# A decoder step in fp32 on one core: the sampled tokens' output projection and second MLP product as unsplit matmuls in two column tiles, with their weights in the ring of gathered keys

## The chip, the cores and the metric

The kernel runs on one core of a Trainium2 chip. TensorE (PE) multiplies, VectorE (DVE), ScalarE (ACT) and GpSimd (POOL) work on elements, and SyncE (SP) issues most of the DMA. The metric is the device time of one execution in microseconds; the median of several runs is compared.

## The reference

One step of a one-layer decoder trunk, all in fp32, for a prompt of 2048 new tokens and 64 sampled tokens (8 sequences of 8) with 8192 past tokens each in a paged cache. Each token goes through a forgetting attention and a matrix-memory recurrence; what follows is this, with a model width of 1024 and a hidden width of 4096:

```python
mix = jnp.concatenate([fox_h, mn.astype(x.dtype)], axis=-1) @ w_o
x1 = _layer_norm(DN_ALPHA * x + mix, ln1_g, ln1_b)
hid = jnp.square(jax.nn.relu(x1 @ w1))
return _layer_norm(DN_ALPHA * x1 + hid @ w2, ln2_g, ln2_b)
```

The outputs are the last line for prompt and sampled tokens, and the new keys, values and states, which the change doesn't touch.

## The kernel before

**Precision.** Most products run as three matmuls on split operands. ACT writes the high part of a tile (`split_hi`, line 154), DVE the rest (`split_lo`, line 157), and `mm3` adds `wh`x`xh`, `wh`x`xl` and `wl`x`xh` in PSUM (lines 163 to 165). The attention of the sampled tokens and a few others multiply f32 tiles without a split; in the trace such a matmul leaves two records on PE.

**Order of the program.** Input projections and recurrence of the prompt come first, then the prompt's attention, its output projection, and then the MLP (`phase_c`). Beside the prompt's work runs the attention of the sampled tokens, in small steps that `tick` issues after so and so much estimated PE time. Its gathered keys land in a ring `kT` of three times two slots of 128x1024 f32 (512 KB), its values in `vt` and `xr`.

**The MLP.** It goes through four blocks of tokens, `CB`, ci = 0 to 3: four tiles of 128 prompt tokens each, and in the last block a fifth tile, 16, with the 64 sampled tokens. So the last block is W = 576 tokens wide, and its first product streams in two pieces of 288. The hidden width is cut into 8 pairs of chunks, p = 0 to 7. `hidden(p, half)` computes relu(x1 w1) squared of 256 hidden columns for the block into a buffer `hq` (PSUM tile `ph`). `output(p, ...)` then does the second product of the pair. For the block's 512 prompt tokens this is a scheme with seven products instead of eight: sums of activations (`s`, and `hq` in place, line 1379) times sums of weights (`dw2`, made beforehand and read from memory). `operands` makes each product's operands on demand, and a product is 12 matmuls of 128x512 into `py` tiles, four PSUM buffers for all. The order of the products is 1, 5, 6, 3, 7, 2, 4. Before a product is issued, those up to two later have their operands made (`order[:at_ + 3]`). `add` (line 1351) adds a PSUM tile into the rows `y`, and in the last block, when a row is complete, issues its statistics (line 1359) and its norm (lines 184 to 193).

**The sampled tokens in it.** Tile 16 isn't part of the seven products. Its activations are split on their own (`hsh`, `hsl`), and after products 1, 5, 3 and 2, whose right-hand operands are quarters of W2 or, for 5, the sum of two, six matmuls of its own ("extra") use the weights `wh`, `wl` that are there, with 64 columns of the array, and DVE adds the result to its row (five adds per pair: product 1's goes into one half and, as 5 holds a sum, off the other).

**The sampled output projection.** `sampled()` is called in the middle of `hidden(7, 1)` of the third block (ci = 2), after the products of p = 6 and ahead of those of p = 7. It loads the mixed activations `mxs`, splits them, and for four blocks of 256 columns loads two pieces of W_O each through `wr`, the ring of five raw weight buffers, splits them, and does 24 matmuls of 64x256. DVE takes them into `y` (line 1300), with the statistics and the norm behind. SP loads the weights in the order in which the program asks for them, and each load waits there for its buffer.

**Buffers.** `wr` has five, `wh` and `wl` four each, `py` four, `ph` two. Engines take their instructions in program order; the operands of the next products and hidden chunks are made ahead of the matmuls by as much as these rings allow.

Of the kernel before, what the change touches and what calls it, by code (L numbers as in the profile page):

```python
# [10 lines left out]
F32 = mybir.dt.float32  # L11
F32R = mybir.dt.float32r
I32 = mybir.dt.int32
AF = mybir.ActivationFunctionType
OP = mybir.AluOpType
# [37 lines left out]
def body(ctx, tc, I, O, stages):  # L53
# [54 lines left out]
    last = {}  # L108
# [44 lines left out]
    def split_hi(dst, src, scale=1.0):  # L153
        last["ACT"] = A.activation(dst, src, AF.Copy, scale=scale)  # L154

    def split_lo(dst, src, hi, eng=None):
        r = (eng or V).tensor_tensor(dst, src, hi.bitcast(F32), op=OP.subtract)  # L157
        if eng is None:
            last["DVE"] = r
        return r  # L160

    def mm3(ps, wh, wl, xh, xl, first, stop, shared=False):
        T.matmul(ps, wh, xh, start=first, stop=False, skip_group_check=shared)  # L163
        T.matmul(ps, wh, xl, start=False, stop=False, skip_group_check=shared)  # L164
        last["PE"] = T.matmul(ps, wl, xh, start=False, stop=stop, skip_group_check=shared)  # L165

    def layer_norm(x, np_, g, b, wk, tg, eng=None):
        st = wk.tile([128, 2, 6], F32, name="ln_st")
# [934 lines left out]
    def raw():  # L1103

        return pcw.tile([128, 1024], F32, name="wr", bufs=5)
# [165 lines left out]
    def phase_c():  # L1271
# [5 lines left out]
        def vecs(l):  # L1277
            g = bcast(I[f"ln{l}_g"], 0, D, f"g{l}", pcw, tag="wr", bufs=5)
            b = bcast(I[f"ln{l}_b"], 0, D, f"b{l}", pcw, tag="wr", bufs=5)
            return g, b  # L1280

        def sampled():

            gb = vecs(1)
            mx = ph.tile([128, 8, 64], F32, name="mxs", tag="s", bufs=1)
            SY.dma_start(mx, dmv[:, :, S:])
            mh = ph.tile([128, 8, 64], F32R, name="mhs", tag="hh", bufs=3)
            ml = ph.tile([128, 8, 64], F32R, name="mls", tag="hl", bufs=3)
            split_hi(mh, mx)
            split_lo(ml, mx, mh)  # L1290
            y = row()
            SY.dma_start(y[:64], x_of(16))
            for c in range(4):
                ps = ppc.tile([128, 512], F32, name="py", bufs=4)[:64, :256]
                for kg in range(2):
                    wh, wl = piece(wo[kg * 512:kg * 512 + 512, c * 256:c * 256 + 256].rearrange("(k p) c -> p k c", p=128))
                    for k in range(4):
                        mm3(ps, mh[:, kg * 4 + k], ml[:, kg * 4 + k], wh[:, k], wl[:, k], kg + k == 0, kg + k == 4)
                s = slice(c * 256, c * 256 + 256)
                V.scalar_tensor_tensor(y[:64, s], y[:64, s], ALPHA, ps, op0=OP.mult, op1=OP.add)  # L1300
                if c == 0:
                    st = pc.tile([128, 2, 6], F32, name="ln_s2", bufs=5)
                if c % 2:
                    V.bn_stats(st[:64, c // 2], y[:64, c * 256 - 256:c * 256 + 256])
            C["normed"] = norm_quick(y[:64], 64, st, *gb, pc, dx1[S:], SY)
# [11 lines left out]
        for ci, blk in enumerate(CB):  # L1317
# [45 lines left out]
            def operands(p):  # L1363
# [10 lines left out]
                    return h, l  # L1374

                def w(src):
                    return piece(src.rearrange("p (k c) -> p k c", k=2))

                v = lambda o, x, y, op: V.tensor_tensor(o, x, y, op=op)

# [12 lines left out]
                             4: lambda: (split(a22), w(dw2[p, 3]))}[n]()  # L1393
                    return r

                hs = []
                if W > 512:
                    for f in (f1, f2):
                        x = f[:, :, 512:576]
                        h = ph.tile([128, 2, 64], F32R, name="hsh", bufs=2)  # L1400
                        l = ph.tile([128, 2, 64], F32R, name="hsl", bufs=2)
                        split_hi(h, x)
                        split_lo(l, x, h)
                        hs.append((h, l))
                return made, hs

            def output(p, ahead, begun=None):
                made, hs, ops = ahead
                if p == 0:
                    for t in blk:  # L1410
# [6 lines left out]
                plan = {1: ("X", True, False, 0, 0, ADD), 5: ("Z", True, False, 2, 1, ADD), 6: ("X", False, False, 0, 1, SUB),  # L1417
                        3: ("Z", False, True, 0, 1, ADD), 7: ("X", False, False, 2, 1, SUB), 2: ("Y", True, True, 0, 0, ADD),
                        4: ("X", False, True, 2, 0, ADD)}
                extra = {1: (0, ((0, ADD), (1, SUB))), 5: (0, ((1, ADD),)), 3: (1, ((1, ADD),)), 2: (1, ((0, ADD),))}  # L1420
                order = (1, 5, 6, 3, 2, 7, 4) if ci == 3 and p == 7 else (1, 5, 6, 3, 7, 2, 4)
                for at_, n in enumerate(order):
                    kind, first_, last_, r0, half, op = plan[n]
                    if p == 7 and at_ == 2 and ci == 3:
# [1 line left out]
                    for m in order[:at_ + 3]:  # L1426
                        if m not in ops:
                            ops[m] = made(m)
                    (h, l), (wh, wl) = ops[n]
                    for i in range(2):  # L1430
                        if kind == "X":
                            ps = X[i]
# [11 lines left out]
                        if begun and at_ < 4:  # L1444
                            turn(ci + 1, at_, i, begun)
                    if n in extra and hs:
                        e, halves = extra[n]
                        ps = ppc.tile([128, 512], F32, name="ph", tag="ph", bufs=2)[:64]
                        for k in range(2):
                            mm3(ps, hs[e][0][:, k], hs[e][1][:, k], wh[:, k], wl[:, k], k == 0, k == 1)  # L1450
                        for q, op in halves:
                            add(16, q, ps, op)
                        tick(1.28)
                if begun:
                    for hf in range(2):
# [11 lines left out]
            def ahead(p, *ns):  # L1467
                made, hs = operands(p)
                r = made, hs, {}
                for n in ns:  # L1470
                    r[2][n] = made(n)
                return r
# [3 lines left out]
            for p in range(8):  # L1476
                pre = []
                if p < 7:
                    hidden(p + 1, 0, lambda: pre.append(ahead(p, 1, 5)))
                else:  # L1480
                    pre.append(ahead(p, 1))
                if p == 6:
# [455 lines left out]
```

## Time and profile before

| | |
|---|---|
| median of three runs | 3253.03 us (3247.86 to 3255.45) |
| the profiled execution | 3243.8 us, span of its core 3241.8 us |
| PE busy | 3132.6 us (97%) |
| DVE, ACT, POOL busy | 2105.9 (65%), 1502.6 (46%), 916.0 us (28%) |
| HBM read and written | 677.71 and 86.38 MB |

The profile is one execution. Busy time of PE counts its pipelined matmuls as one another's continuation, so a busy PE says that it was never without a matmul in flight. In the views of time, a row has its start in us from the span's start, its duration, the engine, the line, the operation, the tile written and those read, their size, and how many like it follow one another; in brackets stands the idle time ahead and what ended it. In lines of groups, the busy total and the mean of one in ns stand behind the first bar, the idle time ahead of them behind the second.

### The profile page before, as it was taken

The page shows a single profiled execution, that of the slowest core. Times are in us where ns is not written, and L with a number is a line of the kernel's source. Part 1 is how long each engine was busy: PE and PEld are TensorE (multiplying, and loading weights), DVE is VectorE, ACT ScalarE, POOL GpSimd, SP SyncE. Part 2 cuts the span into 40 slices and gives each one's busy share as a digit, 9 for nine tenths or more (in the row PEclk, how much of TensorE's full clock was granted, in tenths as well). Part 3 has the DMA queues.
Part 4 walks back from the last instruction along what each step waited for, and adds up shares of the span by engine and source line. Part 5 has one row for each costly group of instructions (what it writes and reads, how often), then busy time and mean ns, then how long its engine had stood idle before and what let it go on. Part 6 is the DMA issues. An engine that isn't in the chain of part 4 may idle for free.

```text
span 3241.8 us, 58017 instructions
## 1 busy us (share of the span) xinstructions
PE 3132.6 (97%) x21681; PEld 2552.5 (79%) x21681; DVE 2105.9 (65%) x5083; ACT 1502.6 (46%) x2965; POOL 916.0 (28%) x974
## 2 busy tenths in 40 slices
PE   8999999999899999999999999999999999899997
PEld 8898999999866667677677777677777777788895
DVE  6856557465488887543556568565686666866658
ACT  4343344334388888412444445343453444544442
POOL 0121324333333333475333324333334121000000
PEclk9999999999999999999999999999999999999998
DMA  5565866777676865686787869778879566543332
GB/s 189 147 214 168 263 216 243 255 244 264 195 257 169 203 177 126 223 297 243 291 297 268 305 241 335 296 265 313 295 282 342 201 231 215 188 164 119 116 105 100
DMA packets 339777, 734.36 MB, mean 227 GB/s; under 512 B 63656, under 2 KB 177704, under 8 KB 338600
## 3 DMA queue, kind: packets, MB, share of 16 engines
q1 hardware_dynamic: 252360, 416.18, 39.7%
q0 software_dynamic: 83520, 304.12, 26.6%
q10 hardware_dynamic: 3616, 10.36, 0.9%
q8 instruction: 171, 2.80, 0.3%
q14 instruction: 110, 0.90, 0.1%
HBM read 677.71 MB, written 86.38 MB: 236 GB/s over the span
## 4 chain that ended last, share of the span: by engine, by line
PE 44%; DMA 4%; DVE 3%; issue 1%; POOL 0%; ACT 0%; DVEq 0%; ACTq 0%; POOLq 0%
PE ph L163 8%; PE ph L164 7%; PE ph L165 7%; PE py L163 6%; PE py L165 5%; PE py L164 5%; PE sO L1790 3%; DMA vt<-cache_v,idxV 2%; PE sQ L1678 2%; DMA xr<-cache_v,idxV 1%; DVE y L1351 1%; DVE wl L157 1%; PE sT L1747 1%; DMA kT<-cache_k,idxK 0%; POOL vt L1766 0%
## 5 line engine op out<-in xcount | busy, mean ns | idle before, releaser
L157 DVE TENSOR_TENSOR wl<-wr,wh 128x1024 fp32r<-128x1024 f32 x364 | 444.2, 1222 | 376.3 <-ACT wh L154 374.9
L154 ACT ACTIVATE wh<-wr 128x1024 fp32r<-128x1024 f32 x364 | 383.0, 1054 | 331.2 <-PE ph L164 175.7
L163 PE MATMUL ph<-x1h,wh 128*128 128x512 f32 (+1 forms) x1280 | 455.0, 355 | 1.1 <-ACT hq L1333 1.1
L164 PE MATMUL ph<-x1l,wh 128*128 128x512 f32 (+1 forms) x1280 | 452.5, 354 | 0.2 <-DVE x1l L157 0.2
L165 PE MATMUL ph<-x1h,wl 128*128 128x512 f32 (+1 forms) x1280 | 450.1, 353 | 0.0
L1655 POOL DMA_INDIRECT kT<-cache_k,idxK x256 | 275.6, 1077 | 536.3 <-PE sQ L1678 470.5
L163 PE MATMUL py<-wh,hh 128*128 128x512 f32 x896 | 357.3, 401 | 3.0 <-ACT hh L154 1.5
L164 PE MATMUL py<-wl,hh 128*128 128x512 f32 x896 | 352.5, 393 | 3.4 <-DVE wl L157 3.4
L165 PE MATMUL py<-wh,hl 128*128 128x512 f32 x896 | 350.0, 394 | 2.0 <-DVE hl L157 2.0
L1351 DVE TENSOR_TENSOR y<-y,py 128x512 f32<-128x512 f32 x416 | 280.6, 681 | 64.0 <-PE py L165 59.3
L163 PE MATMUL pm<-xh,whi 128*128 128x256 f32 (+1 forms) x1024 | 298.9, 292 | 0.0
L164 PE MATMUL pm<-xl,whi 128*128 128x256 f32 (+1 forms) x1024 | 294.8, 288 | 0.0
L165 PE MATMUL pm<-xh,wlo 128*128 128x256 f32 (+1 forms) x1024 | 293.8, 287 | 0.0
L1766 POOL DMA_INDIRECT vt<-cache_v,idxV x164 | 180.3, 1100 | 384.4 <-PE sO L1790 315.3
L163 PEld LDWEIGHTS ph<-x1h,wh 128*128 128x128 f32 x1280 | 240.4, 188 | 42.0 <-issue 7.8
L164 PEld LDWEIGHTS ph<-x1l,wh 128*128 128x128 f32 x1280 | 240.5, 188 | 33.8 <-issue 3.3
L165 PEld LDWEIGHTS ph<-x1h,wl 128*128 128x128 f32 x1280 | 240.1, 188 | 34.1 <-issue 3.7
L163 PE MATMUL pm<-whi,xh 128*128 128x256 f32 (+2 forms) x816 | 236.9, 291 | 9.2 <-ACT whi L154 8.2
L164 PE MATMUL pm<-wlo,xh 128*128 128x256 f32 (+2 forms) x816 | 232.5, 285 | 0.6 <-DVE wlo L157 0.6
L165 PE MATMUL pm<-whi,xl 128*128 128x256 f32 (+2 forms) x816 | 232.2, 285 | 0.0
L998 ACT ACTIVATE S<-S,mx 128x512 f32<-128x512 f32 (+2 forms) x320 | 207.8, 653 | 19.0 <-DVE mx L984 17.6
L163 PEld LDWEIGHTS py<-wh,hh 128*128 128x128 f32 x896 | 168.6, 189 | 51.4 <-issue 10.9
(372 smaller groups left out, 6799.7 us busy)
## 6 DMA issues: line engine op xcount, KB each, us to landing
wr<-w SPq DMA_DIRECT2D x224, 512.0 KB
wr<-dw SPq DMA_DIRECT2D x128, 512.0 KB
wra<-w_in SPq DMA_DIRECT2D x104, 512.0 KB
dw<-w POOLq DMA_DIRECT2D x48, 512.0 KB, 8.4
Rb<-dR SPq DMA_DIRECT2D x128, 128.0 KB
xn<-xp_t SPq DMA_DIRECT2D x16, 512.0 KB
qn<-dq SPq DMA_DIRECT2D x128, 64.0 KB
kn<-k_prompt SPq DMA_DIRECT2D x64, 128.0 KB
```

The lines of the kernel that those rows point to most:

```text
L154: last["ACT"] = A.activation(dst, src, AF.Copy, scale=scale)
L157: r = (eng or V).tensor_tensor(dst, src, hi.bitcast(F32), op=OP.subtract)
L163: T.matmul(ps, wh, xh, start=first, stop=False, skip_group_check=shared)
L164: T.matmul(ps, wh, xl, start=False, stop=False, skip_group_check=shared)
L165: last["PE"] = T.matmul(ps, wl, xh, start=False, stop=stop, skip_group_check=shared)
L998: last["ACT"] = A.activation(sp[:, :w], sp[:, :w], AF.Exp, bias=mx[:, 7:8], accum_out=lp[:, k:k + 1])
L1351: V.tensor_tensor(y, y, ps, op=op)
L1655: G.indirect_dma_start(out=piece(n), out_offset=None, in_=ck, in_offset=IO(ap=idxK[:, b, j // 2, j % 2:j % 2 + 1], axis=0))
L1678: r = T.matmul(pq[h4 * 32:h4 * 32 + 32, hg].rearrange("p (k c) -> p k c", k=2), z["qb"][:, hd], kv, start=(db == 0), stop=(db == 1), skip_ ...
L1747: T.transpose(p[:, f], z["U"][u][:, hg, f].rearrange("p k t -> p (k t)"), ident)
L1766: vx["last"] = G.indirect_dma_start(out=vt.rearrange("p f c -> p (f c)"), out_offset=None, in_=cv, in_offset=IO(ap=idxV[:, b, (kt % 4) * 4 ...
L1790: after_ = T.matmul(po[r:r + 32], z["PT"][:, hg, 2 * f + g, pg].rearrange("p h q -> p (h q)"), vts[f][:, g, hg * 256:(hg + 1) * 256], star ...
```

## The change

- A helper `two_sides` issues two unsplit f32 matmuls, one into PSUM partitions 0 to 63 and one into 64 to 127, each in 64 columns of the array.
- The sampled output projection uses them: the upper half of the reduction goes into one half of the tile, the lower into the other, and DVE adds both into `y`, with two instructions where it had one. The mixed activations and W_O are no longer split. W_O's eight pieces land in the slots of the key ring `kT` (`spare`), six of which are there.
- The products of p in the last block take their raw weights from the key ring too, and keep them (`wr` in `ops`); the sampled tile's part runs from these and from `hq` directly, in two groups of four instead of four groups of six: after product 2 with the weights of 1 and 2, after product 3 with those of 5 and 3. The splits into `hsh` and `hsl` are gone.
- In the last block the order is 1, 2, 5, 3, 6, 7, 4 for all p, and products 1 and 2 are the ones made ahead.

```diff
@@ -163,6 +163,11 @@
         T.matmul(ps, wh, xh, start=first, stop=False, skip_group_check=shared)
         T.matmul(ps, wh, xl, start=False, stop=False, skip_group_check=shared)
         last["PE"] = T.matmul(ps, wl, xh, start=False, stop=stop, skip_group_check=shared)
+
+    def two_sides(ps, sides, first, stop):
+
+        for n, (w, x) in enumerate(sides):
+            last["PE"] = T.matmul(ps[n * 64:n * 64 + 64], w, x, start=first, stop=stop, skip_group_check=True)
 
     def layer_norm(x, np_, g, b, wk, tg, eng=None):
         st = wk.tile([128, 2, 6], F32, name="ln_st")
@@ -1279,25 +1284,31 @@
             b = bcast(I[f"ln{l}_b"], 0, D, f"b{l}", pcw, tag="wr", bufs=5)
             return g, b
 
+        turn_ = [0]
+
+        def spare():
+
+            turn_[0] += 1
+            return kx["ring"][:, turn_[0] // 2 % 3, turn_[0] % 2]
+
         def sampled():
 
             gb = vecs(1)
             mx = ph.tile([128, 8, 64], F32, name="mxs", tag="s", bufs=1)
             SY.dma_start(mx, dmv[:, :, S:])
-            mh = ph.tile([128, 8, 64], F32R, name="mhs", tag="hh", bufs=3)
-            ml = ph.tile([128, 8, 64], F32R, name="mls", tag="hl", bufs=3)
-            split_hi(mh, mx)
-            split_lo(ml, mx, mh)
             y = row()
             SY.dma_start(y[:64], x_of(16))
             for c in range(4):
-                ps = ppc.tile([128, 512], F32, name="py", bufs=4)[:64, :256]
+                ps = ppc.tile([128, 512], F32, name="py", bufs=4)[:, :256]
+                w = []
                 for kg in range(2):
-                    wh, wl = piece(wo[kg * 512:kg * 512 + 512, c * 256:c * 256 + 256].rearrange("(k p) c -> p k c", p=128))
-                    for k in range(4):
-                        mm3(ps, mh[:, kg * 4 + k], ml[:, kg * 4 + k], wh[:, k], wl[:, k], kg + k == 0, kg + k == 4)
+                    w.append(spare().rearrange("p (k c) -> p k c", k=4))
+                    SY.dma_start(w[kg], wo[kg * 512:kg * 512 + 512, c * 256:c * 256 + 256].rearrange("(k p) c -> p k c", p=128))
+                for k in range(4):
+                    two_sides(ps, [(mx[:, kg * 4 + k], w[kg][:, k]) for kg in range(2)], k == 0, k == 3)
                 s = slice(c * 256, c * 256 + 256)
-                V.scalar_tensor_tensor(y[:64, s], y[:64, s], ALPHA, ps, op0=OP.mult, op1=OP.add)
+                V.scalar_tensor_tensor(y[:64, s], y[:64, s], ALPHA, ps[:64], op0=OP.mult, op1=OP.add)
+                V.tensor_tensor(y[:64, s], y[:64, s], ps[64:128], op=OP.add)
                 if c == 0:
                     st = pc.tile([128, 2, 6], F32, name="ln_s2", bufs=5)
                 if c % 2:
@@ -1374,7 +1385,9 @@
                     return h, l
 
                 def w(src):
-                    return piece(src.rearrange("p (k c) -> p k c", k=2))
+                    wr = (spare() if W > 512 else raw()).rearrange("p (k c) -> p k c", k=2)
+                    SY.dma_start(wr, src.rearrange("p (k c) -> p k c", k=2))
+                    return (*piece(None, wr), wr)
 
                 v = lambda o, x, y, op: V.tensor_tensor(o, x, y, op=op)
 
@@ -1393,16 +1406,10 @@
                              4: lambda: (split(a22), w(dw2[p, 3]))}[n]()
                     return r
 
-                hs = []
-                if W > 512:
-                    for f in (f1, f2):
-                        x = f[:, :, 512:576]
-                        h = ph.tile([128, 2, 64], F32R, name="hsh", bufs=2)
-                        l = ph.tile([128, 2, 64], F32R, name="hsl", bufs=2)
-                        split_hi(h, x)
-                        split_lo(l, x, h)
-                        hs.append((h, l))
+                hs = [f[:, :, 512:576] for f in (f1, f2)] if W > 512 else []
                 return made, hs
+
+            order = (1, 2, 5, 3, 6, 7, 4) if W > 512 else (1, 5, 6, 3, 7, 2, 4)
 
             def output(p, ahead, begun=None):
                 made, hs, ops = ahead
@@ -1417,8 +1424,7 @@
                 plan = {1: ("X", True, False, 0, 0, ADD), 5: ("Z", True, False, 2, 1, ADD), 6: ("X", False, False, 0, 1, SUB),
                         3: ("Z", False, True, 0, 1, ADD), 7: ("X", False, False, 2, 1, SUB), 2: ("Y", True, True, 0, 0, ADD),
                         4: ("X", False, True, 2, 0, ADD)}
-                extra = {1: (0, ((0, ADD), (1, SUB))), 5: (0, ((1, ADD),)), 3: (1, ((1, ADD),)), 2: (1, ((0, ADD),))}
-                order = (1, 5, 6, 3, 2, 7, 4) if ci == 3 and p == 7 else (1, 5, 6, 3, 7, 2, 4)
+                extra = {2: (1, ((0, 0, ADD), (0, 1, SUB), (1, 0, ADD))), 3: (5, ((0, 1, ADD), (1, 1, ADD)))}
                 for at_, n in enumerate(order):
                     kind, first_, last_, r0, half, op = plan[n]
                     if p == 7 and at_ == 2 and ci == 3:
@@ -1426,7 +1432,7 @@
                     for m in order[:at_ + 3]:
                         if m not in ops:
                             ops[m] = made(m)
-                    (h, l), (wh, wl) = ops[n]
+                    (h, l), (wh, wl, wr) = ops[n]
                     for i in range(2):
                         if kind == "X":
                             ps = X[i]
@@ -1444,12 +1450,13 @@
                         if begun and at_ < 4:
                             turn(ci + 1, at_, i, begun)
                     if n in extra and hs:
-                        e, halves = extra[n]
-                        ps = ppc.tile([128, 512], F32, name="ph", tag="ph", bufs=2)[:64]
+                        e, parts = extra[n]
+                        ps = ppc.tile([128, 512], F32, name="ph", tag="ph", bufs=2)
+                        w = ops[e][1][2], wr
                         for k in range(2):
-                            mm3(ps, hs[e][0][:, k], hs[e][1][:, k], wh[:, k], wl[:, k], k == 0, k == 1)
-                        for q, op in halves:
-                            add(16, q, ps, op)
+                            two_sides(ps, [(hs[i][:, k], w[i][:, k]) for i in range(2)], k == 0, k == 1)
+                        for i, q, op in parts:
+                            add(16, q, ps[i * 64:i * 64 + 64], op)
                         tick(1.28)
                 if begun:
                     for hf in range(2):
@@ -1476,7 +1483,7 @@
             for p in range(8):
                 pre = []
                 if p < 7:
-                    hidden(p + 1, 0, lambda: pre.append(ahead(p, 1, 5)))
+                    hidden(p + 1, 0, lambda: pre.append(ahead(p, *order[:2])))
                 else:
                     pre.append(ahead(p, 1))
                 if p == 6:
```

How this moves the instructions is seen at three places. The rows give the line, the operation, the tile written and those read, and the size as stationary columns by moving columns.

On PE, the sampled output projection in before: behind the transposes (`px`) stand 96 split matmuls into `py` with `mhs`, `mls`, and behind them product 1 of p = 7 (`wh`, `hh`).

```order
L1166 MATMUL px_30467<-ident,xr 128x128 x4
L163 MATMUL py<-wh,mhs 64x256
L164 MATMUL py<-wl,mhs 64x256
...
L165 MATMUL py<-wh,mls 64x256
L163 MATMUL py<-wh,hh 128x512 x2
```

And after, at the same place: `kT` is W_O in the key ring.

```order
L1171 MATMUL px_30363<-ident,xr 128x128 x4
L170 MATMUL py<-kT,mxs 64x256 x24
L1171 MATMUL px_30377<-ident,xr 128x128 x4
L170 MATMUL py<-kT,mxs 64x256
L163 MATMUL py<-wh,hh 128x512
...
L165 MATMUL py<-wh,hl 128x512
L170 MATMUL py<-kT,mxs 64x256 x7
L163 MATMUL py<-wh,hh 128x512 x2
```

Three column blocks stand as one run of 24 matmuls; the fourth has one ahead of product 1 and seven behind it.

On DVE behind it in before: the last column block's add (line 1300), statistics, the norm, and then the operands of product 5 (`hl` of `s`, `wl`).

```order
L157 TENSOR_TENSOR wl<-wr,wh 128x1024 x2
L1300 SCALAR_TENSOR_TENSOR y<-y,py 64x256
L1304 BN_STATS ln_s_30266<-y 64x6
L184 BN_AGGR ln_m_30383<-ln_s_30266 64x2
L186 TENSOR_SCALAR ln_r_30385<-ln_m_30383 64x1
L190 SCALAR_TENSOR_TENSOR y<-y,ln_m_30383,g_30216 64x512 x2
L192 SCALAR_TENSOR_TENSOR y<-y,ln_r_30385,b_30218 64x512 x2
L157 TENSOR_TENSOR hl<-s,hh 128x512
L157 TENSOR_TENSOR wl<-wr,wh 128x1024
```

And after:

```order
L1310 SCALAR_TENSOR_TENSOR y<-y,py 64x256
L1392 TENSOR_TENSOR s<-hq 128x512
L1311 TENSOR_TENSOR y<-y,py 64x256
L1392 TENSOR_TENSOR hq<-hq 128x2x256
L1315 BN_STATS ln_s_30237<-y 64x6
L1392 TENSOR_TENSOR hq<-s,hq 128x2x256
L189 BN_AGGR ln_m_30279<-ln_s_30237 64x2
L191 TENSOR_SCALAR ln_r_30281<-ln_m_30279 64x1
L195 SCALAR_TENSOR_TENSOR y<-y,ln_m_30279,g_30216 64x512 x2
L197 SCALAR_TENSOR_TENSOR y<-y,ln_r_30281,b_30218 64x512 x2
L157 TENSOR_TENSOR hl<-s,hh 128x512
L157 TENSOR_TENSOR wl<-wr,wh 128x1024
```

The sums `s` and `hq` for the next products, which stood earlier among the splits of W_O, now stand between the last column block's two adds and its norm; the operands of product 5 are behind the norm in both.

On PE in one period of the last block after the change, the sampled tile's matmuls (`ph` from `kT` and `hq`) stand in one run between products' matmuls, the group of products 1 and 2 and that of 5 and 3 next to each other.

```order
L164 MATMUL py<-wl,hh 128x512
L165 MATMUL py<-wh,hl 128x512
L170 MATMUL ph<-kT,hq 64x512 x8
L163 MATMUL py<-wh,hh 128x512
L164 MATMUL py<-wl,hh 128x512
```

In before the same place in a period had one of four groups such as this, with two of each kind:

```order
L165 MATMUL py<-wh,hl 128x512
L163 MATMUL ph<-wh,hsh 64x512
L164 MATMUL ph<-wl,hsh 64x512
L165 MATMUL ph<-wh,hsl 64x512
...
L163 MATMUL py<-wh,hh 128x512
```

## The prediction

> **What bounds the kernel now.** I read the page first, then the busy time of five stretches from the sampled output projection to the end, then the waits and three repeating periods inside the longest stretch.
>
> ```profile
> span 3241.8 us, 58017 instructions
> PE 3132.6 (97%) x21681; PEld 2552.5 (79%) x21681; DVE 2105.9 (65%) x5083; ACT 1502.6 (46%) x2965; POOL 916.0 (28%) x974
> 2769.60:2817.00 47.40, 37.72 (x220) 31.02 (x218) 43.44 (x64) 25.03 (x33) 1.00 (x1) 0.96 0.65 222
> 2831.00:3197.00 366.00, 365.99 (x2208) 325.96 (x2209) 233.84 (x314) 168.53 (x271) 1.44 (x1) 1.00 0.39 127
> 3197.00:3219.50 22.50, 22.37 (x98) 16.56 (x96) 22.50 (x36) 6.61 (x10) 0.00 (x0) 1.00 0.13 44
> 2959.49:3009.57 50.08, 50.08 (x302) 44.42 (x301) 31.99 (x45) 22.61 (x38) 0.00 (x0) 1.00 0.36 116
> PE ph L163 <- ACT hq L1333: 1.1, 1, 1.1
> ```
>
> PE is busy for 97% of the span, so only what shortens PE's own list, or a place where PE waits, can move the end. The stretch rows give length, then busy time (and instructions) of PE, weight loads, DVE, ACT, POOL, then granted clock, DMA share and GB/s. The change touches three of them. From 2831 to 3197 the last token block runs and PE is the limit without remainder: 365.99 of 366.00 us busy, one wait of 1.1 us in all. It repeats once for each pair of hidden chunks, and one period is 50.08 us with PE busy in all of it and DVE in 31.99. From 2769.6 to 2817, with the sampled output projection, PE is busy in only 37.72 of 47.40, so waits decide there. After 3197 DVE is busy in 22.50 of 22.50: the tail is DVE's.
>
> **The steady periods: four groups become one block.** In before, each pair of chunks has four groups of six split matmuls for the sampled tile.
>
> ```profile
> 2959.27 0.39 PE L165 MATMUL py<-wh,hl 128*128 128x512 f32 x1
> 2959.49 0.40 PE L163 MATMUL ph<-wh,hsh 128*64 128x512 f32 x1
> ...
> 2960.87 0.39 PE L163 MATMUL py<-wh,hh 128*128 128x512 f32 x1
> L163 PE MATMUL ph<-wh,hsh 128*64 128x512 f32 x8 | 3.1, 393 | 0.0
> ```
>
> One group lasts from 2959.49 to 2960.87, 1.38 us for six matmuls at 0.23 from start to start; the group row (one period) has eight `wh,hsh` matmuls, two for each group, so there are four groups and 4 x 1.38 = 5.52 us of PE a period. In their place comes one block of eight unsplit matmuls in two column tiles, and the trace has no such matmul with 512 columns. Its price comes from three others:
>
> ```profile
> 1000.15 1.95 PE L1020 MATMUL po<-PT,vn 128*64 128x256 f32 x16
> 1002.03 0.66 PE L1011 MATMUL pt<-ident,S 128*128 128x128 f32 x4
> 269.65 1.12 PE L844 MATMUL mm<-vx,kws 64*128 64x512 f32 x2
> 270.70 0.39 PE L163 MATMUL pm<-xh,whi 128*128 128x256 f32 x1
> 2743.95 0.39 PE L165 MATMUL py<-wh,hl 128*128 128x512 f32 x1
> 2744.27 1.07 PE L1790 MATMUL sO<-vt,PTs 128*32 128x256 f32 x16
> 2745.27 0.50 PE L163 MATMUL py<-wh,hh 128*128 128x512 f32 x1
> 2745.61 0.40 PE L164 MATMUL py<-wl,hh 128*128 128x512 f32 x1
> ```
>
> An unsplit f32 matmul leaves two records. At 256 columns in two column tiles (`po`, 128x64 tiles), 16 records, eight matmuls, take 1.88 us up to the next instruction, about 0.22 for each pair of records: two tiles run together there. One tile alone at 512 columns (`mm`) has its two records in 1.05 us up to the next instruction's start (269.65 to 270.70): two steps of 0.43, twice the 0.22 of 256 columns, and 0.2 for the change of shape. If the two tiles overlap at 512 columns as they do at 256, eight matmuls are 16 records in 8 steps of 0.43 = 3.44 us. What the way into and out of column tiles costs, the `sO` block shows: the gap ahead is 2744.27 - 2743.95 = 0.32 where 0.23 is usual, the first matmul behind it lasts 0.34 to the next where 0.23 is usual, and its last step carries about 0.14 more; that is 0.34 us a block. The new block is then 3.44 + 0.34 = 3.78 us and saves 5.52 - 3.78 = 1.74 a period.
>
> From this comes what the new order brings as waits. ACT's and DVE's splits of the sampled activations go (DVE is idle for 18 of the 50 us anyway), the number of adds into the sampled rows stays at five, and the raw weights stay readable in the key ring, which nothing else uses then. What is tight is the four-buffer ring of `wh` and `wl`: product 2 now runs second and product 6 fifth, so the first W1 piece of the next hidden chunk waits for the buffer that product 6 or 3 frees, with ACT's 1.05 us and DVE's 1.22 us of split behind it. Written out by hand with the trace's durations, PE waits 0 to 0.2 us there, once a period. I take 0.1, so 1.65 a period. Seven periods (p = 0 to 6) lie in the stretch in which PE is the limit: 7 x 1.65 = **11.6 us**. The ends are 7 x 1.2 = 8.4 (a wait of half a microsecond) and 7 x 1.74 = 12.2.
>
> The Trainium skill, "TensorE: Matmul & The Clock Gate", in the table of Part 3 on packing, gives three column tiles only 2.38 times the rate of one, some 0.79 of a full overlap; an estimate by it is 3.44 / 0.79 + 0.34 = 4.7 us for the block, and a sum of some 9 us instead of 15. This case's trace has two tiles at a full overlap for 256 columns (the `po` row), and none shows it for 512; what a partial overlap would do here is the second rival below.
>
> **The output projection.** These rows carry it, PE's and then DVE's, ACT's and SP's.
>
> ```profile
> 2769.61 0.36 PE L163 MATMUL py<-wh,mhs 128*64 128x256 f32 x1
> 2780.67 0.33 PE L164 MATMUL py<-wl,mhs 128*64 128x256 f32 x1 [0.68 <-DVE wl L157]
> 2783.57 0.73 PE L163 MATMUL py<-wh,hh 128*128 128x512 f32 x2 [1.44 <-ACT wh L154]
> 2790.68 0.50 PE L164 MATMUL py<-wl,hh 128*128 128x512 f32 x1 [2.85 <-DVE wl L157]
> 2791.28 0.63 PE L163 MATMUL py<-wh,hh 128*128 128x512 f32 x1
> 2784.70 0.41 DVE L1300 SCALAR_TENSOR_TENSOR y<-y,py 64x256 f32<-64x256 f32 x1
> 2785.14 0.69 DVE L1304 BATCH_NORM_STATS2 ln_s<-y 64x6 f32<-64x512 f32 x1
> 2786.16 1.40 DVE L190 SCALAR_TENSOR_TENSOR y<-y,ln_m,g 64x512 f32<-64x512 f32 x2
> 2787.49 1.40 DVE L192 SCALAR_TENSOR_TENSOR y<-y,ln_r,b 64x512 f32<-64x512 f32 x2
> 2789.41 1.21 DVE L157 TENSOR_TENSOR wl<-wr,wh 128x1024 fp32r<-128x1024 f32 x1
> 2771.73 3.68 SPq L1137 DMA_DIRECT2D wr<-w_o  x2
> 2774.97 1.06 ACT L154 ACTIVATE wh<-wr 128x1024 fp32r<-128x1024 f32 x1 [0.53 <-DMA wr<-w_o]
> L157 DVE TENSOR_TENSOR wl<-wr,wh 128x1024 fp32r<-128x1024 f32 x8 | 9.7, 1208 | 0.0
> ```
>
> The projection holds PE from 2769.61 to about 2782, then PE waits 1.44 us, 0.53 and 2.85, the last for the `wl` of product 5, which lies behind the sampled row's norm on DVE and ends at 2790.6. From there to 2817 DVE has no gap (the last row, of 2790.6 to 2816.9, shows eight `wl` and no idle time ahead of any), so how early that `wl` ends sets how early the next stretch begins.
>
> Now: column blocks 0 to 2 are 24 unsplit matmuls in pairs of tiles, 24 x 0.22 = 5.2 us, to about 2774.9. The last two W_O pieces wait for a free key slot, which block 0 gives at about 2771.6; the row of SP and that of ACT behind it show a W_O piece readable 3.2 us after its issue at 2771.73, so 2774.9, and SP's next loads (product weights of the last block) queue behind and are not due for 10 us. Block 3's first matmul, product 1 (12 x 0.23 = 2.7), block 3's other seven (1.6) and transposes put block 3's end at about 2780.3. Then DVE goes in order: an add and a second add of 0.4, `s` and two `hq` of 0.68, statistics 0.69 and 0.3, the norm 2 x 1.4 less overlap, `hl` 0.6, `wl` 1.14, in all 7.7 us, so 2788.0 instead of 2790.6. **2.6 us** earlier. Behind it both have the same work. The ends: PE also comes back at 0.63 us a matmul for some time after its wait (the row of 2791.28), and a longer wait, 7.7 us, may double that stretch, by 2 us, though DVE covers it; the loads could come 2 to 4 us late, as no row shows how a load lands when it is issued beside two others from HBM. So from -6 to +2 us.
>
> The Trainium skill, "TensorE: Matmul & The Clock Gate", Part 1, says that an idle window of about 3.4 us halves the array's clock and that as long a busy one restores it. The trace agrees: matmuls at 0.43 us from start to start for about 3 us from 2791.28. By the page the longer wait costs the same as the shorter, no more.
>
> **The tail.** DVE decides, from 3196 to its last norm.
>
> ```profile
> 3198.30 0.29 DVE L157 TENSOR_TENSOR hsl<-hq,hsh 128x128 fp32r<-128x128 f32 x1
> 3237.14 1.40 DVE L192 SCALAR_TENSOR_TENSOR y<-y,ln_r,b 128x512 f32<-128x512 f32 x2
> ```
>
> For p = 7 DVE loses its last split of sampled activations (0.29; the other is earlier) and keeps its other adds, norms and splits; product 2 comes earlier, so three sampled sums end sooner and less is left behind the last product. By hand DVE's solid run is 41 to 42 us where it was 42.6 (3195.96 to 3238.54): **0.7 us** less, with ends +1 and -1.7.
>
> The sum is 11.6 + 2.6 + 0.7 = 14.9 us. Against the profiled execution's own time of 3243.8 us that is 3229; against the median of 3253.0 shown, 9.2 us above that execution and itself inside 3247.9 to 3255.5, it is **3238 us**.
>
> **Rivals.**
> 1. *The tiles do not run together at 512 columns.* Nothing in the trace has two tiles at 512; `po` at 256 speaks against it. Then the block is 16 x 0.43 + 0.34 = 7.2 us instead of 5.5, 1.7 more for 7 periods, +12 us, and the projection 64 records x 0.22 = 13.8 instead of 12, +1 to +3. About +14, or 3266, slower. It decides from a step of 0.65 us for a pair of records on.
> 2. *The overlap is partial*: a pair of records at a step halfway from 0.43 to the 0.65 of rival 1, 0.54. The block is 8 x 0.54 + 0.34 = 4.7 us and saves 0.8, less 0.1 of wait: 5 us in seven periods, and 3 elsewhere: 3245. The `po` row speaks against it, the twice longer stream for it. The packing table named above is the rule that would make it so.
> 3. *The weight ring or DVE becomes the bound* in the periods: the wait for `wl` of W1 eats all of the 1.74. DVE's 18 idle us a period speak against it, the four buffers for it. Only projection and tail remain: 3250, the same.
> 4. *The last two W_O pieces are late*, and SP's queue behind them: the projection gives nothing, and may lose 2 us. 11.6 + 0.7 - 2 = 10: 3243.
>
> **Numbers.** Forecast 0.72, rival 1 0.06, 2 0.06, 3 0.09, 4 0.07. 0.2% of this time, what a measurement of this kernel can tell from no change, is 6.5 us. Faster: all of the forecast but a 0.02 corner (8.4 with both other terms bad, 5.4 us), five sixths of rival 2, rival 4 but for 0.01: 0.81. Slower: rival 1 and 0.01 of rival 3: 0.07. Same: 0.12. The range goes from all terms at their best (12.2 + 6 + 1.7 = 20, and 5 of run spread): 3228, to rival 3: 3252. Left out are rival 1 and some of the ends.
>
> **What would show it.** A period of 48.4 us for the last block, with one `ph` block of 3.8 us on PE and no wait above 0.2; the `wl` of product 5 ending about 2788; the tail's DVE run near 42 us. I am wrong if pairs of records at 512 columns are 0.6 us or more apart, if PE shows a wait for `wl` or `wh` of a microsecond in each period, or if the stretch of the projection isn't shorter.

## The result and the profile after

Over 14 runs each the median went from 3252.77 us to 3241.82 us (3233.26 to 3251.06): 11.0 us less, a ratio of 0.997 with a 95% interval of 0.9961 to 0.9979. A second set beside a new set of before gave 0.9964 (0.995 to 0.9978). The forecast was 14.9 us less and 3238 us, with 3228 to 3252 as its range: the sign, the mechanism and the range hold, and the gain is three quarters of what the sum gave.

The two profiled executions taken alone would say that nothing was gained. This is the head of the page of after:

```profile
span 3242.4 us, 57713 instructions
PE 3127.7 (96%) x21585; PEld 2535.8 (78%) x21585; DVE 2095.6 (65%) x5062; ACT 1489.0 (46%) x2940; POOL 907.2 (28%) x974
```

Its span is 0.6 us longer than that of before. But the first matmul of the sampled output projection starts at 2781.49 us in it and at 2769.61 in before, and up to there PE has the same 19065 records in the same order in both (ACT and DVE too, but for the last few of each, where before splits the projection's operands). So 11.9 us of that comparison lie ahead of the change, and I compare from this matmul on. The rows are busy times by stretch, with the columns of the stretch rows in the prediction: first from that matmul to the first matmul of the last block, then from there to the end of the span; two rows of before, two of after with one period of the last block as a third, and two of the second profile of after.

```profile
2769.61:2816.97 47.36, 37.68 (x219) 30.98 (x217) 43.43 (x64) 25.02 (x33) 1.00 (x1) 0.96 0.65 222
2816.97:3241.74 424.77, 401.35 (x2402) 355.26 (x2400) 287.31 (x409) 181.19 (x289) 11.45 (x9) 0.98 0.37 122
```

```profile
2781.49:2827.38 45.89, 35.18 (x186) 25.44 (x185) 37.53 (x61) 17.07 (x25) 1.00 (x1) 0.89 0.69 240
2827.38:3242.41 415.03, 392.05 (x2337) 338.74 (x2336) 287.51 (x392) 175.39 (x273) 9.36 (x9) 0.98 0.33 117
3015.12:3063.84 48.72, 48.69 (x294) 42.22 (x293) 32.01 (x42) 21.79 (x34) 0.00 (x0) 1.00 0.33 119
```

```profile
2774.00:2819.84 45.84, 34.26 (x186) 24.55 (x185) 37.51 (x60) 16.87 (x25) 1.00 (x1) 0.93 0.70 241
2819.84:3234.52 414.68, 392.21 (x2338) 338.89 (x2336) 287.72 (x393) 175.26 (x273) 9.35 (x9) 0.98 0.33 117
```

The two stretches together take 472.1 us in before, 460.9 and 460.5 in the two profiles of after: 11.2 and 11.6 us less, which agrees with the medians. The projection's stretch gives 1.5 of it, and the last block and tail 9.7 to 10.1. A period is 48.72 us where it was 50.08, so seven periods at this price give 9.5. In the first profile of after two of them are longer (49.14 and 48.80), in the second none is.

The tail can be read by itself, from ACT's last square of p = 7 to the end of DVE's last row:

```profile
3196.29 0.45 ACT L1334 ACTIVATE hq<-hq 128x288 f32<-128x288 f32 x1
3197.36 0.45 ACT L1345 ACTIVATE hq<-hq 128x288 f32<-128x288 f32 x1
3236.14 2.73 DVE L197 SCALAR_TENSOR_TENSOR y<-y,ln_r,b 128x512 f32<-128x512 f32 x4
```

The first row is of before, where DVE ends at 3238.54 (the prediction shows its last row): 42.25 us. The other two are of after: 41.51 us, 0.7 less. But the span ends 3.2 us behind DVE's last row in before and 3.55 in after, so 0.3 of that is lost again at the end.

PE around the sampled tile's new block in one period of after:

```profile
3019.00 0.39 PE L165 MATMUL py<-wh,hl 128*128 128x512 f32 x1
3019.32 3.65 PE L170 MATMUL ph<-kT,hq 128*64 128x512 f32 x16
3022.90 0.50 PE L163 MATMUL py<-wh,hh 128*128 128x512 f32 x1
3023.24 0.40 PE L164 MATMUL py<-wl,hh 128*128 128x512 f32 x1
```

Sixteen records from 3019.32 to 3022.90, with a gap of 0.32 ahead and a first matmul of 0.34 behind: from 3019.00 to 3023.24 are 4.24 us where two steps of 0.23 would stand without the block, so it costs 3.78 us, the figure forecast.

What the forecast took for 0.1 us is in the next two sets of rows, PE's and DVE's behind the block in the same period:

```profile
3031.45 0.29 PE L163 MATMUL ph<-x1h,wh 128*128 128x288 f32 x1
3031.58 0.29 PE L164 MATMUL ph<-x1l,wh 128*128 128x288 f32 x1
3031.91 0.40 PE L165 MATMUL ph<-x1h,wl 128*128 128x288 f32 x1
3030.03 0.69 DVE L1362 TENSOR_TENSOR y<-y,py 128x512 f32<-128x512 f32 x1
3030.64 1.22 DVE L157 TENSOR_TENSOR wl<-wr,wh 128x1024 fp32r<-128x1024 f32 x1
```

The first matmul that needs the low part `wl` of the W1 piece starts 0.33 us after the one ahead, where 0.13 is the step, and the one behind it, at 3032.15, is late by another 0.1: DVE finishes that `wl` at 3031.86. PE counts as busy through most of it, since the earlier matmuls are still in the pipeline, so the list of waits shows nothing; only the starts do.

PE and then DVE in the sampled output projection of after:

```profile
2781.49 5.40 PE L170 MATMUL py<-kT,mxs 128*64 128x256 f32 x48
2786.82 0.66 PE L1171 MATMUL px<-ident,xr 128*128 128x128 f32 x4
2787.40 0.65 PE L170 MATMUL py<-kT,mxs 128*64 128x256 f32 x2
2790.93 1.94 PE L170 MATMUL py<-kT,mxs 128*64 128x256 f32 x14
2794.64 0.73 PE L163 MATMUL py<-wh,hh 128*128 128x512 f32 x2 [1.77 <-ACT hh L154]
2800.91 0.80 PE L164 MATMUL py<-wl,hh 128*128 128x512 f32 x1 [5.54 <-DVE wl L157]
2801.50 0.63 PE L165 MATMUL py<-wh,hl 128*128 128x512 f32 x1
2806.62 0.44 PE L163 MATMUL py<-wh,hh 128*128 128x512 f32 x1
2792.91 0.41 DVE L1310 SCALAR_TENSOR_TENSOR y<-y,py 64x256 f32<-64x256 f32 x1 [5.08 <-PE py L170]
2797.72 1.40 DVE L197 SCALAR_TENSOR_TENSOR y<-y,ln_r,b 64x512 f32<-64x512 f32 x2
2799.65 1.21 DVE L157 TENSOR_TENSOR wl<-wr,wh 128x1024 fp32r<-128x1024 f32 x1
```

DVE now sits idle for 5.08 us until the fourth column block is through, and then does sums, norm and operands while PE waits 1.77 and 5.54 us. Product 5's `wl` ends 19.4 us after the projection's start, where before needed 21.0.

### The profile page after: what moved, and what is told of

Same layout as the page of the kernel before. It is cut to its first block, busy times and chain, and to the rows that moved or that the text cites. A ratio compares the mean times of both kernels' runs of the same rounds, so it can differ in the third digit from the quotient of the medians.

```text
span 3242.4 us, 57713 instructions
## 1 busy us (share of the span) xinstructions
PE 3127.7 (96%) x21585; PEld 2535.8 (78%) x21585; DVE 2095.6 (65%) x5062; ACT 1489.0 (46%) x2940; POOL 907.2 (28%) x974
## 5 line engine op out<-in xcount | busy, mean ns | idle before, releaser
L157 DVE TENSOR_TENSOR wl<-wr,wh 128x1024 fp32r<-128x1024 f32 x300 | 366.0, 1222 | 249.5 <-ACT wh L154 241.9
L154 ACT ACTIVATE wh<-wr 128x1024 fp32r<-128x1024 f32 x300 | 315.4, 1053 | 290.1 <-PE ph L164 162.4
```

## The experiments

In all of them the time is read from the projection's first matmul on, or from one period of the last block, and not from the whole time: all but `best` and `after_again` were timed once, and the unchanged part ahead of the projection varies by more than what is looked for. The rows are stretches as above, and `...` marks what a shown edit leaves out.

**Each half alone.** `proj_only` is before with the new projection:

```diff
 def sampled():
-    wh, wl = piece(wo[...])
-    mm3(ps, mh[:, kg * 4 + k], ml[:, kg * 4 + k], wh[:, k], wl[:, k], kg + k == 0, kg + k == 4)
+    w.append(spare().rearrange("p (k c) -> p k c", k=4))
+    two_sides(ps, [(mx[:, kg * 4 + k], w[kg][:, k]) for kg in range(2)], k == 0, k == 3)
...
```

> Only the sampled output projection is changed; the sampled tile's second product stays split, in the old order and with its weights in the old ring. Measured by the trace from the projection's first matmul: 47.4 us to the first matmul of the last block in before, 45.9 in after. If the projection's gain is its own, 45.9 here and periods of 50.07 as before. If instead the loads of the last block's weights through the key ring matter for it, between 46 and 48.

```profile
2780.30:2826.14 45.84, 35.26 (x185) 25.54 (x185) 37.51 (x60) 17.10 (x25) 1.00 (x1) 0.89 0.54 172
3017.55:3067.62 50.07, 50.07 (x302) 44.42 (x301) 31.98 (x44) 22.61 (x36) 0.00 (x0) 1.00 0.37 116
```

`extras_only` is after with the old `sampled()`:

```diff
 def sampled():
-    two_sides(ps, [(mx[:, kg * 4 + k], w[kg][:, k]) for kg in range(2)], k == 0, k == 3)
+    mm3(ps, mh[:, kg * 4 + k], ml[:, kg * 4 + k], wh[:, k], wl[:, k], kg + k == 0, kg + k == 4)
...
```

> Only the sampled tile's second product is changed, with order and key ring; the output projection is split as before. If the two parts are independent: 47.4 us from the projection's first matmul to the last block, periods of 48.72 as after. If the projection's early end is what lets the last block start well, the first period is longer, later ones are not.

```profile
2773.67:2820.57 46.90, 37.87 (x220) 31.02 (x217) 43.66 (x64) 25.14 (x34) 1.00 (x1) 0.96 0.69 225
2959.20:3007.92 48.72, 48.69 (x294) 42.22 (x293) 32.01 (x42) 21.79 (x34) 0.00 (x0) 1.00 0.36 120
```

The parts are independent. The projection's gain is its own, 45.84 with periods as before; the period's gain is the second product's own, 48.72 with a projection of 46.90, half a microsecond from the 47.36 of before, a difference that no run explains.

**Do two column tiles overlap at 512 columns?** `one_tile` sends both matmuls of each pair into the same 64 columns:

```diff
-two_sides(ps, [(hs[i][:, k], w[i][:, k]) for i in range(2)], k == 0, k == 1)
+for i in range(2):
+    T.matmul(ps[:64], hs[i][:, k], w[i][:, k], start=k + i == 0, stop=k + i == 2, ...)
...
-add(16, q, ps[i * 64:i * 64 + 64], op)
+add(16, q, ps[:64], op)
```

> The eight unsplit matmuls of a period all go into the same 64 columns, so no two can run together (the sums that come out are not the sampled tile's; adds, loads and order are those of after). Overlap theory: the block grows from 3.8 us by eight steps of 0.43 to 7.2, and a period from 48.72 to 51.9 to 52.2, slower than before's 50.07. Rival, that the array isn't what limits a pair and a block costs the same in one tile: 48.7.

A period, and PE at the block:

```profile
3019.02:3071.15 52.13, 52.10 (x294) 43.25 (x294) 32.22 (x41) 21.78 (x34) 0.00 (x0) 1.00 0.35 111
3031.12 7.08 PE L1458 MATMUL ph<-kT,hq 128*64 128x512 f32 x16
3038.14 0.50 PE L163 MATMUL py<-wh,hh 128*128 128x512 f32 x1
```

The same sixteen records take 7.02 us in one tile and 3.58 in two, 1.96 times, and the period is 52.13 us, 2.1 more than in before. So the whole gain of the periods hangs on the second tile: unsplit matmuls alone would have been slower than the split ones.

**What makes the 0.3 us of wait?** Four runs. `addless` leaves out the sampled add that subtracts, 0.6 us of DVE:

```diff
-extra = {2: (1, ((0, 0, ADD), (0, 1, SUB), (1, 0, ADD))), 3: ...}
+extra = {2: (1, ((0, 0, ADD), (1, 0, ADD))), 3: ...}
...
```

> After, with one of the five sampled adds of a period left out (the one that subtracts), 0.6 us of DVE. The period of after is 48.72 where block for block 48.34 was worked out, and PE waits 0.3 us in each for the low part of a W1 piece. Theory, DVE's run of work without a gap behind the block makes it late: the wait goes and the period is 48.35 to 48.45. Rival, the four buffers of the weight ring (or the product order) hold it: 48.7 as after.

`order_only` is before with the new order of products in the last block:

```diff
-order = (1, 5, 6, 3, 2, 7, 4) if ci == 3 and p == 7 else (1, 5, 6, 3, 7, 2, 4)
+order = (1, 2, 5, 3, 6, 7, 4) if W > 512 else (1, 5, 6, 3, 7, 2, 4)
...
```

> Before, with only the order of products in the last block changed to 1, 2, 5, 3, 6, 7, 4 (the sampled tile stays in four groups of split matmuls, its weights in the old ring). In after a period is 48.72 us where the block alone would make 48.34, and PE waits 0.3 us for the low part of a W1 piece. If the order brings that wait, by the buffers it keeps longer: a period of 50.3 to 50.5 here. If the block of unsplit matmuls brings it: 50.07 as before.

`hh4` and `ring5` are after with a longer ring each, and a shorter one of raw weights to make room:

```diff
-h = ph.tile([128, 2, 256], F32R, name="hh", bufs=3)
-l = ph.tile([128, 2, 256], F32R, name="hl", bufs=3)
-return pcw.tile([128, 1024], F32, name="wr", bufs=5)
+h = ph.tile([128, 2, 256], F32R, name="hh", bufs=4)
+l = ph.tile([128, 2, 256], F32R, name="hl", bufs=4)
+return pcw.tile([128, 1024], F32, name="wr", bufs=4)
...
```

> After, with four buffers instead of three for the split activations hh and hl, and four instead of five raw weight buffers to make room. Leaving out an add (0.6 us of DVE) left the period at 48.70, so DVE's run isn't the cause of the 0.3 us. Theory now: ACT's high part of an activation waits for a buffer that a product's end frees (0.23 us behind PE), and the W1 piece stands behind it in ACT's order; with a fourth buffer the period is 48.35 to 48.45. Rival, the weight ring wh, wl holds the W1 piece: 48.7. With a raw buffer less, loads may also come late: over 48.8.

```diff
-wh = C["pc"].tile([128, 1024], F32R, name="wh", bufs=4)
-wl = C["pc"].tile([128, 1024], F32R, name="wl", bufs=4)
-return pcw.tile([128, 1024], F32, name="wr", bufs=5)
+wh = C["pc"].tile([128, 1024], F32R, name="wh", bufs=5)
+wl = C["pc"].tile([128, 1024], F32R, name="wl", bufs=5)
+return pcw.tile([128, 1024], F32, name="wr", bufs=3)
...
```

> After, with five buffers instead of four for the split weights wh and wl, and three instead of five raw weight buffers to make room. Neither an add less, nor the order alone, nor a fourth activation buffer took the 0.3 us of wait away. Theory, the W1 piece's low part waits for its buffer in the weight ring: a period of 48.35 to 48.45. Rival, the piece is late because of where ACT and DVE have it in their order, which stands whatever the ring: 48.7. With two raw buffers fewer, earlier stretches may lose some microseconds.

One period each of `addless`, `order_only` and `hh4`, with a line of the waits of the last, and two of `ring5`, with a row of DVE and three of PE in the first:

```profile
3009.32:3058.02 48.70, 48.66 (x294) 42.21 (x293) 31.41 (x41) 21.79 (x34) 0.00 (x0) 1.00 0.35 119
```

```profile
3017.68:3067.75 50.07, 50.07 (x302) 44.41 (x301) 32.31 (x44) 22.75 (x36) 0.00 (x0) 1.00 0.37 116
```

```profile
3013.69:3063.28 49.59, 48.70 (x294) 42.22 (x293) 32.16 (x42) 21.77 (x34) 0.00 (x0) 1.00 0.36 117
PE ph L165 <- DVE wl L157: 0.9, 1, 0.9
```

```profile
3027.20:3075.60 48.40, 48.40 (x294) 42.18 (x293) 31.97 (x42) 21.60 (x34) 0.00 (x0) 1.00 0.37 120
3075.60:3124.00 48.40, 48.40 (x294) 42.17 (x293) 31.98 (x42) 21.67 (x34) 0.00 (x0) 1.00 0.37 120
3041.52 1.22 DVE L157 TENSOR_TENSOR wl<-wr,wh 128x1024 fp32r<-128x1024 f32 x1
3043.58 0.29 PE L163 MATMUL ph<-x1h,wh 128*128 128x288 f32 x1
3043.71 0.30 PE L164 MATMUL ph<-x1l,wh 128*128 128x288 f32 x1
3043.84 0.29 PE L165 MATMUL ph<-x1h,wl 128*128 128x288 f32 x1
```

My first theory fell: DVE with 0.6 us less of work in a period (31.41 for 32.01) leaves the period at 48.70. A fourth activation buffer doesn't help either: the same matmul then waits 0.9 us for the same low part. Whether that comes from the raw buffer less or from the order in which things are issued with such a ring, these runs don't tell, so the second theory gets no support from it, and isn't excluded either. The order of the products by itself costs nothing (50.07). With a fifth weight buffer the wait is gone: DVE ends the low part at 3042.74, 1.1 us ahead of the matmul that reads it, the three matmuls start 0.13 us apart, and the period is 48.40, 0.32 less. Other periods of that run were 48.6 to 49.3 us long; in those with a wait on PE, ACT stood 7.5 us or more for a product's weights from memory, where it stood 6.1 in the period shown. So a longer weight ring takes the wait away, even with two raw buffers fewer. The way in which it does is open: in after ACT isn't seen waiting for a buffer right ahead of that piece, it splits it at once behind an activation; with the fifth buffer ACT has the piece one place earlier in its list. Nor do the runs part the shorter block from the key ring as what brings the wait out; the order alone doesn't. The run is no better version: its one time was 3256.31 us.

**The projection's chain.** `wo_wr` lands the last two W_O pieces in the raw ring:

```diff
-w.append(spare().rearrange("p (k c) -> p k c", k=4))
+w.append((spare() if c < 3 else raw()).rearrange("p (k c) -> p k c", k=4))
```

> After, with the last two W_O pieces in the ring of raw weights instead of the key ring, where they need not wait for the first column block. Block 3 then follows block 2 at once, and DVE's idle 5.1 us ahead of block 3's add goes. Theory, that add starts the chain that ends with product 5's low part: from the projection's start to the last block 41.5 to 43 us instead of 45.9. Rival, with two raw buffers taken the weights of products 5 to 7 land late and PE waits for these instead: 45 to 47.

The stretch, PE around it and DVE's add of the last column block:

```profile
2776.68:2818.24 41.56, 33.52 (x185) 24.99 (x184) 37.46 (x60) 18.42 (x27) 1.00 (x1) 0.90 0.73 266
2781.91 1.90 PE L170 MATMUL py<-wr,mxs 128*64 128x256 f32 x16
2791.89 0.80 PE L164 MATMUL py<-wl,hh 128*128 128x512 f32 x1 [4.21 <-DVE wl L157]
2783.88 0.41 DVE L1310 SCALAR_TENSOR_TENSOR y<-y,py 64x256 f32<-64x256 f32 x1 [0.86 <-PE py L170]
```

The fourth block follows the third at once, DVE's add comes 7.2 us after the start instead of 11.4, and the stretch is 41.56 us: 4.3 less, as that start of the chain gives. The rest of the program then takes 415.39 us, 0.7 more than in the second profile of after.

`normfree` takes away only the rule that puts the norm ahead of what the last pair issues:

```diff
-if "normed" in C:
-    es_.enter_context(tc.issue_after(C.pop("normed").ins))
+C.pop("normed", None)
```

> After, without the order that puts the sampled row's norm ahead of what the last pair of the third block issues; nothing else is changed. Product 5's low part need not wait for 2.7 us of norm and 1.4 us of sums. Theory, these stand in PE's way: 42 to 44 us instead of 45.9 from the projection's start to the last block. Rival, DVE has the same work in all and no gap from there to the last block, so order among it is worth nothing: 45.5 to 46.5. Turns of the next block that come between may make it later: over 46.5.

```profile
2782.43:2822.13 39.70, 32.98 (x179) 23.34 (x179) 34.29 (x56) 16.32 (x25) 1.00 (x1) 0.96 0.75 265
2796.81 0.50 PE L163 MATMUL py<-wh,hh 128*128 128x512 f32 x1 [1.54 <-ACT hh L154]
2797.15 0.40 PE L164 MATMUL py<-wl,hh 128*128 128x512 f32 x1
```

39.70 us, 6.2 less and more than expected: product 5's operand is there when PE comes to it (the second row follows the first without a wait), and other work of DVE fills the time in which it sat idle ahead of the last column block.

**A version that beats both.** `best` has both edits, and two adds instead of five, one column tile for each half of the output, with the plain quarter of W2 loaded for the right half:

```diff
+if m == 5 and hs:
+    ops["x"] = raw().rearrange("p (k c) -> p k c", k=2)
+    SY.dma_start(ops["x"], I["w2"][p, 1].rearrange("p (k c) -> p k c", k=2))
...
-if n in extra and hs:
+if n == 3 and hs:
+    for i, w in enumerate(((ops[1][1][2], ops["x"]), (ops[2][1][2], wr))):
+        for k in range(2):
+            two_sides(ps, [(hs[i][:, k], w[j][:, k]) for j in range(2)], i + k == 0, i + k == 2)
+    for q in range(2):
+        add(16, q, ps[q * 64:q * 64 + 64], ADD)
```

> After, with three further changes: the last two W_O pieces in the raw ring (41.6 us from the projection's start to the last block where after had 45.9), no forced order of the sampled norm (39.7 alone), and two adds in place of five for the sampled tile, as one column tile gathers all of the left half of the output and the other all of the right, with the plain quarter of W2 loaded for it. If the first two add up: 36 to 38 us; rival, both take the same idle time of DVE: 39 to 41. Periods 48.7 as an add less changed nothing, and 1.2 to 1.8 us less in the tail, which is DVE's. In all 8 to 10 us less than after, 18 to 21 less than before: a ratio of 0.9935 to 0.995.

> After unchanged, beside the best version on the same chip: 10 to 12 us less than before, ratio 0.9963 to 0.997, periods of 48.72, and 45.9 us from the projection's start to the last block.

```profile
2775.70:2813.38 37.68, 32.34 (x184) 24.09 (x184) 34.94 (x56) 16.47 (x26) 2.03 (x1) 1.00 0.79 279
2813.38:3224.00 410.62, 390.28 (x2338) 337.17 (x2336) 274.63 (x372) 175.74 (x274) 9.61 (x9) 0.99 0.37 129
2999.15:3047.85 48.70, 48.66 (x294) 42.21 (x293) 30.22 (x39) 21.78 (x34) 0.00 (x0) 1.00 0.39 130
```

The median is 3232.85 us, with 3242.75 for after and 3254.07 for before on the same chip; a ratio of 0.9934 (0.9921 to 0.9948). The stretch of the projection is 8.2 us shorter than after's 45.84, inside the 36 to 38 us expected, though the two edits do not add up in full (4.3 and 6.2). A period is 48.70, as an add less had told. The last block and tail are 4.1 us shorter than in the second profile of after. By the same marks as above 2.0 of it is DVE's tail, a little more than the 1.2 to 1.8 expected of three adds fewer at the end, and 1.4 lies between the first matmul of that block and ACT's last square of its first pair, which was neither forecast nor taken apart.

## Why the prediction was right, and where its sizes were off

- **The block's price** (5.52 to 3.78 us, 1.74 a period) held to the last digit. It came from the step of a pair at 256 columns, doubled, and from the `sO` block's way in and out; the gap ahead (0.32) and the first matmul behind (0.34) are the same in both blocks, so the figure isn't luck. Rivals 1 and 2 are excluded: sixteen records in 3.58 us are 0.45 for a pair, way out included, where rival 2 had 0.54, and `one_tile` shows what no overlap gives (7.02 us). The Trainium skill, "TensorE: Matmul & The Clock Gate", Part 3, has 2.38 times for three column tiles; here two give 1.96 times, close to two, so the measurement decides against taking that loss over to two.
- **The wait for the weight ring**, "0 to 0.2 us there, once a period. I take 0.1", is the term that was too small: 0.32 by `ring5` (48.72 to 48.40), 0.2 us more than taken in each of seven periods. The place was right, the low part of the first W1 piece, and a longer ring of `wh` and `wl` takes the wait away, as the forecast's mechanism has it. Period by period the gain was 1.35 instead of 1.65, so 9.5 us instead of 11.6. Of the 1.74 the last 0.06 or so isn't accounted for: 50.08 less 48.40 is 1.68. Rival 3, the ring eating all of it, had this mechanism at five times the price.
- **The projection**, 2.6 us, gave 1.5. The fourth column block ended later than the sum had it: DVE's add for it came 11.4 us after the start, where 10.7 was worked out, as the switches of tile shape (0.3 us each, `px` to `kT`, `kT` to `wh`, and back) were left out; and the chain behind it took 7.95 for 7.7. Rival 4 isn't borne out: in after PE shows no wait for the pieces when it comes to them. What they cost is their place in the order, 4.3 us by `wo_wr`. The sum held this place as given and did not see that it could be changed.
- **The clock** behind the long wait. The prediction had an end in which the slow stretch doubles, and a sentence by which it stays the same. In the first profile of after, 12 matmuls run at 0.43 from start to start, 5.1 us, behind a wait of 5.54 (the rows of 2801.50 and 2806.62), where before had 8 in 3.4 us behind 2.85. But in the second profile of the same program only 6 do, 2.6 us (2794.02 to 2796.58), behind the same wait of 5.54. The Trainium skill, "TensorE: Matmul & The Clock Gate", Part 1, gives about 3.4 us of work to come back; the two profiles lie on either side of it. That DVE covers this, as was assumed, shows: the stretch is 45.89 us with the long slow part and 45.84 with the short one, and DVE has no gap in it behind product 5's `wl`.
- **The tail**, 0.7 us, held: 42.25 us became 41.51. What the sum had nothing for is the end of the span behind it, 0.3 later.

The sum was 14.9 and the runs show 11.0 to 11.6: 2.1 less in the periods, 1.1 less in the projection, and 0.3 at the very end.

## What to carry to other kernels

In this kernel unsplit f32 matmuls with 64 stationary columns were worth it only in pairs on two column tiles, and their price could be read from packed blocks that the trace had already: pairs times step (0.43 us at 512 columns), and 0.34 us for the way in and out. Where a change takes work from the engine that sets the pace, look at which ring of buffers was just long enough, since the time that is taken out is first given to the next wait, and a wait as short as this one (0.33 us for 0.13 between two starts) shows only in the starts of the matmuls, not in the list of waits. Compare profiles from the first instruction that differs: the part ahead of it may differ by more than the change. And read each part by its own marks: a part that is only what is left of a difference collects the errors of the others.

## What was not expected of the hardware

The same instructions of PE in the same order up to the projection took 2769.6 us in the profile of before and 2781.5 and 2774.0 in those of after, so an unchanged stretch may vary by 12 us, more than the change brought, while three periods of the last block of before repeat within 0.01 us. And behind the same wait of 5.54 us the array ran at about half its rate (0.43 us from start to start for 0.23) for 5.1 us in one profile of after and for 2.6 in the other.
